# Gate and up projection: units 2 and 3 unit by unit, with their last products halved as in the later units

## The chip, the cores and the metric

The kernel runs on one core of a Trainium2 chip. The metric is the device time of one execution in microseconds (us). Five engines work side by side, each through a queue of its own in a fixed order: TensorE (PE in the profile; its weight loads are PEld), VectorE (DVE), ScalarE (ACT), GpSimd (POOL), and SyncE (SP), which here only issues transfers between HBM (the large memory) and SBUF (the on-chip memory). Matmuls write to PSUM banks, which DVE and ACT read. Engines wait for each other by semaphores.

## The reference

A two-layer encoder on 1024 tokens of width 1024, all in float32. Cut to what matters, one layer does this:

```
h = rmsnorm(x, norm_mix[i])
...                                      # attention (window or grid) and memory attention
x = x + concat(y_tok, y_mem) @ w_out[i]
h = rmsnorm(x, norm_ffn[i])
gu = h @ w_gate_up[i]                    # 1024 x 1024 times 1024 x 5632
x = x + (silu(gu[:, :2816]) * gu[:, 2816:]) @ w_down[i]
```

The change is in the product `h @ w_gate_up`, in both layers.

## The kernel before, in words

Every float32 operand of a matmul is split into a high and a low part. ACT casts the high part (`hi`, L107), DVE subtracts it from the original for the low part (`lo`, L110), and a product takes three matmuls: high by high, high by low, low by high (`three`). So each weight tile costs one ACT and one DVE instruction before TensorE can use it.

Gate and up work on 22 units `us[0..21]` (`Pair`), each 128 gate columns and 128 up columns. A unit's weights and the normalized input are cut into a two-by-two block product that is done with seven products instead of eight (n = 0 to 6 in the code; the words of the change count them from 1). One product is twelve 128x512 matmuls: four blocks of 128 rows by three terms. Right operands `B[n]` are common to all units: for n = 0, 1, 4, 5 they are the tiles `hB`, for n = 2, 3, 6 the tiles `hT8` (shown as `hT`), made by `right_sides` from the normalized x. Left operands are the unit's weights or sums of them, made by POOL (L1061, L1068) in the tile `wS` and then split into a tile of two products: n = 0 and 1 from the raw weights, n = 2 and 3 from the sums in `wS`, n = 4 and 5 from further sums. These overwrite `wS`, so POOL's second pair of subtractions waits until `lo` of the tile for 2 and 3 is done. `wS` has two buffers (tag `S`), the tiles for splits come from `wgu8` (six buffers, first four units, n = 0 and 1), from tag `whl` in lower SBUF (three buffers, shared with other stages) or from tag `w8` in upper SBUF (`wgu2`, one buffer). Products 0, 2, 4, 6 add up in a PSUM bank X, products 1, 3, 5 in a bank Y; after most of them ACT or DVE reads the bank (`read`), before the next product adds to it.

From the third pair on, product 6 of two neighbours is done jointly (`Fourth`): both left tiles and the right operand `B[6]` are halved once more, and seven products of half the rows and half the columns (six 128x256 matmuls each, L1186) take the place of two products of twelve 128x512 matmuls. They stand in three groups, A (two), B (two) and C (three), between the neighbour's last products, in a bank X4 and a bank Y4; DVE subtracts their results (L1214). The last product of C adds to the half of Y4 that DVE has read after B. `quarters` makes the quarter-size right operands (`q4`, `q4h`) and overwrites half of `B[6]`'s first tiles, so it runs when the undivided products 6 are done.

The list `order` fixes the sequence of products. The first four units do products 0 and 1 first, one unit after the other. Units 0 and 1, and then units 2 and 3, do n = 3, 2, 5, 4, 6 in turn, each for both units. The later ones go unit by unit. The loop `gate_up` walks the list; four places ahead of a product it calls `prepare`, which makes its left tile, and then it advances the generators for the right operands, `rest` (`right_sides`) and `more` (`quarters`).

While the first products run, the second half's norm is finished: TensorE adds squares (`st`, L223), DVE adds epsilon (`nv`, L243), POOL takes the power (`nr`, L244), DVE spreads it on a diagonal (`diag`, L252), and TensorE multiplies that by ones (`bc`, L266), after the first product of unit 1. DVE needs `bc` for the right operands of products 2 to 6.

The text fixes what is computed, in which tiles, and what follows what on a tile. The place of an instruction in its engine's queue is set at build time by a scheduler, which places an instruction where it reckons its inputs to be ready and its buffer to be free. On the chip each queue then runs strictly as built.

Of the kernel before, what the change touches and what calls it, by code (L numbers as in the profile page):

```python
# [41 lines left out]
def trunk_kernel(ctx: ExitStack, tc: tile.TileContext, a: dict, out: bass.AP):  # L42
# [63 lines left out]
    def hi(dst, src):  # L106
        return nc.scalar.copy(dst, src)  # L107

    def lo(dst, src, h, eng=None):
        return (eng or nc.vector).tensor_tensor(dst, src, h.bitcast(F32), op=ALU.subtract)  # L110
# [40 lines left out]
    def run_some(g, n):  # L151
        for _ in range(n):
            next(g, None)
# [388 lines left out]
    for layer in range(2):  # L542
# [470 lines left out]
        with (  # L1013
# [32 lines left out]
            class Pair:  # L1046
# [6 lines left out]
                def prepare(self, n):  # L1053

                    n -= n % 2
                    if n in self.left:
                        return
                    g1, g2 = self.raw[0][:, :HS], self.raw[0][:, HS:]
                    if n > 0:
                        u1, u2 = self.raw[1][:, :HS], self.raw[1][:, HS:]  # L1060
                    sub = lambda o, p_, q_: nc.gpsimd.tensor_tensor(o, p_, q_, op=ALU.subtract)  # L1061
                    s = self.raw[0]
                    if n == 2:
                        self.s = fs.tile([P, D], F32, tag="S", name="wS", bufs=2)
                    if n in (2, 4):
                        s = self.s
                    if n == 2:
                        nc.gpsimd.tensor_tensor(s[:, HS:], u1, u2, op=ALU.add)  # L1068
                        sub(s[:, :HS], s[:, HS:], g1)
                    if n == 4:  # L1070
                        sub(s[:, HS:], g1, u1)
                        sub(s[:, :HS], g2, s[:, :HS])
                    if n == 0 and self.j < first:
                        w = fp.tile([P, 2, D], F32R, tag="t8", name="wgu8", bufs=6)
                    elif n == 2 and self.j >= first:
                        w = fp.tile([P, 2, D], F32R, tag="w8", name="wgu2", bufs=1)
                    else:
                        w = wp.tile([P, 2, D], F32R, tag="whl", name="wgu", bufs=3)
                    if n == 6:
                        hi(w[:, 0, :HS], u2)  # L1080
                        lo(w[:, 1, :HS], u2, w[:, 0, :HS])
                    else:
                        hi(w[:, 0], s)
                        lo(w[:, 1], s, w[:, 0])
                    self.left[n], self.left[n + 1] = w[:, :, :HS], w[:, :, HS:]
                    if n == 4:
                        self.left[4], self.left[5] = self.left[5], self.left[4]
                    if n > 3 or (n == 0 and 2 <= self.j < first):
                        load_gu()
# [142 lines left out]
            first = 4  # L1232
            order = [(u, n) for u in us[:first] for n in (0, 1)]
            for j in range(0, NF, 2):
                a_, b_ = us[j : j + 2]
                z = Fourth(a_, b_)
                if j < first:
                    order += [(u, n) for n in (3, 2, 5, 4, 6) for u in (a_, b_)]
                else:
                    order += [(a_, n) for n in range(6)] + [(b_, n) for n in range(4)]  # L1240
                    order += [(z, "A"), (b_, 4), (z, "B"), (b_, 5), (z, "C")]

            loads = [(us[j], 0) for j in range(first)] + [(us[0], 1), (us[1], 1)]
# [3 lines left out]
            def load_gu():  # L1247
                u, i = next(loads, (None, 0))
                if u is not None:
                    u.raw[i] = raw_tile("wgu_raw")  # L1250
                    nc.sync.dma_start(u.raw[i], a["w_gu"][layer, 2 * u.j + i])
# [3 lines left out]
            for f in range(2):  # L1255
                for m in range(NK):
                    n = f * NK + m + 3
# [89 lines left out]
            def hand_over(p, a_, b_):  # L1347


                b11, b12, b21, b22 = a_.c2, a_.c1, b_.c2, b_.c1  # L1350
                sub = lambda p_, q_: nc.vector.tensor_tensor(o, p_, q_, op=ALU.subtract)
                keep(0, p, b11)
                keep(1, p, b21)
                keep(5, p, b22)
                o = t1 = temp("t1")
                sub(b12, b11)
                keep(3, p, t1)
                o = t2 = temp("t2")
                sub(b22, t1)
                keep(2, p, t2)  # L1360
                o = b12
                sub(b22, b12)
                keep(4, p, b12)
                o = temp("t4")
                sub(t2, b21)
                keep(6, p, o)
# [4 lines left out]
            def gate_up():  # L1371
                load_gu()
                for i, (u, n) in enumerate(order):
                    if i + lead < len(order):
                        v, n_ = order[i + lead]
                        v.prepare(n_)
                    u.product(n)
                    u.read(n)
                    if i == 1:
                        norms[1].sums()  # L1380
                    if i > 1:
                        run_some(rest, 2 if i == 2 or i >= 2 * first else 1)
                    if i >= 7 * first - 1:
                        run_some(more, 1)
                    if n == "C":
                        hand_over(u.units[0].j // 2, *u.units)
                    elif n == 6 and u.j % 2:
                        hand_over(u.j // 2, us[u.j - 1], u)
                    yield i - len(order)
# [215 lines left out]
            for to_go in gate_up():  # L1605
                for what, g in ahead.get(to_go, ()):
                    if what is keep_rows:
                        keep_rows(g)
                    elif what is left_side:
                        left_side(0, g, (us[-1].copied, us[-1].summed) if g == 1 else ())  # L1610
                    else:
                        what(0, g)
# [7 lines left out]
            for at_, (i, g) in enumerate(dorder):  # L1620
# [4 lines left out]
                p, n = groups[g]  # L1625
# [128 lines left out]
```

## Time and profile before

| | |
|---|---|
| median of 3 runs | 2112.03 us (2110.97 to 2112.73) |
| the profiled execution | 2112.72 us, its span 2110.9 us |
| TensorE busy in the span | 2092.0 us, 99% |
| VectorE, ScalarE, GpSimd busy | 72%, 51%, 28% |
| mean granted clock of TensorE | 0.998 of full |

How to read the rows shown below: a timeline row has the start in us from the span's beginning, the duration, engine, line of the kernel, operation, result and operands by the program's names without buffer numbers, shapes, and how many instructions are merged (x24); in brackets stands how long the engine had waited and for what. A matmul's shown duration includes its way through the array; two matmuls overlap, so the distance between starts is what PE spends. In a row of windows the columns are the stretch, its length, the busy time and count of PE, PEld, DVE, ACT and POOL, the granted clock, the share of the transfer engines and GB/s. Layer 0 has its gate and up products from 391 us on, layer 1 from 1463 us on.

### The profile page before, as it was taken

What the parts mean: (1) busy time and instruction counts of PE and PEld (TensorE: products, weight loads), DVE (VectorE), ACT (ScalarE), POOL (GpSimd) and SP (SyncE); (2) the same over time, 40 slices, a digit from 0 to 9 for tenths busy, and PEclk for the clock granted to TensorE, in tenths of its full rate; (3) what the DMA queues carried; (4) which work ended last, traced back from release to release, by engine and by line L of the source; (5) the groups of instructions that cost most, each with busy time, mean ns of one, the idle gap of its engine ahead of it and who ended that gap; (6) DMA issues with size and microseconds to landing.
All of it is one profiled execution on the core that took longest, in us unless ns stands there. A gap on an engine that the chain in (4) does not pass through costs nothing.

```text
span 2110.9 us, 29032 instructions
## 1 busy us (share of the span) xinstructions
PE 2092.0 (99%) x10318; PEld 1751.5 (83%) x10318; DVE 1524.3 (72%) x2474; ACT 1076.9 (51%) x2037; POOL 582.7 (28%) x615
## 2 busy tenths in 40 slices
PE   9999999999999999999999999999999999999998
PEld 8788888888888888888888888888788888888886
DVE  7787886897666666866766666677986666678675
ACT  6687785544334335444466666664543434344443
POOL 0344330334434430000233223203343444400001
PEclk9999999999999999999999999999999999999999
DMA  6421138232333227956232222274233333277562
GB/s 233 146 82 51 31 103 283 89 115 101 109 115 110 85 105 281 337 180 206 80 98 68 69 72 78 65 269 155 75 110 105 110 115 105 91 263 280 184 210 94
DMA packets 121776, 288.07 MB, mean 136 GB/s; under 512 B 12704, under 2 KB 21152, under 8 KB 121632
## 3 DMA queue, kind: packets, MB, share of 16 engines
q1 hardware_dynamic: 113744, 272.42, 38.5%
q10 hardware_dynamic: 7888, 13.79, 1.7%
q8 instruction: 82, 1.34, 0.3%
q14 instruction: 62, 0.51, 0.1%
HBM read 211.19 MB, written 68.95 MB: 133 GB/s over the span
## 4 chain that ended last, share of the span: by engine, by line
PE 80%; issue 12%; DVE 3%; POOL 2%; ACT 2%; DMA 1%; SPq 0%; POOLq 0%; ACTq 0%; DVEq 0%
PE X L1104 16%; PE Y L1104 16%; PE mm L141 15%; PE po L141 8%; PE X L1542 5%; PE Y L1542 4%; PE S L746 3%; PE O L812 3%; PE pT L791 3%; PE X L1186 2%; PE Y L1186 2%; PE mm L448 1%; POOL wS L1061 1%; POOL wf L110 1%; DVE wgu L110 0%
## 5 line engine op out<-in xcount | busy, mean ns | idle before, releaser
L1104 PE MATMUL Y<-hB,wgu 128*128 128x512 f32 x1056 | 255.6, 391 | 0.8 <-ACT c L1124 0.8
L1104 PE MATMUL X<-hB,wgu 128*128 128x512 f32 x1056 | 254.9, 391 | 0.0
L1542 PE MATMUL X<-hB,wd 128*128 128x512 f32 (+1 forms) x1092 | 242.9, 383 | 0.0
L110 DVE TENSOR_TENSOR wgu<-wS,wgu 128x1024 fp32r<-128x1024 f32 (+1 forms) x124 | 154.3, 1245 | 120.5 <-ACT wgu L107 120.4
L1542 PEld LDWEIGHTS X<-hB,wd 128*128 128x128 f32 x1092 | 200.2, 188 | 40.1 <-issue 0.5
L1104 PEld LDWEIGHTS Y<-hB,wgu 128*128 128x128 f32 x1056 | 196.8, 188 | 43.4 <-ACT c L1124 1.6
L1104 PEld LDWEIGHTS X<-hB,wgu 128*128 128x128 f32 x1056 | 195.9, 188 | 40.1 <-ACT g L1121 0.2
L776 POOL TENSOR_SCALAR p<-p,stat 128x384 f32<-128x384 f32 (+1 forms) x256 | 141.8, 573 | 302.5 <-DVE stat L773 196.7
L141 PE MATMUL mm<-hT,wqk 128*128 128x512 f32 x672 | 199.2, 405 | 0.0
L107 ACT CAST wgu<-wS 128x1024 fp32r<-128x1024 f32 (+1 forms) x124 | 114.3, 923 | 141.9 <-POOL wS L1061 124.5
L141 PE MATMUL po<-yT,wo 128*128 128x512 f32 x768 | 183.5, 394 | 0.0
L1542 PE MATMUL Y<-hB,wd 128*128 128x512 f32 x792 | 180.2, 389 | 0.0
L1542 PEld LDWEIGHTS Y<-hB,wd 128*128 128x128 f32 x792 | 148.7, 188 | 30.8
L244 POOL TENSOR_TENSOR nr<-nv,neg_half 128x4 f32<-128x4 f32 (+1 forms) x12 | 13.2, 1103 | 582.6 <-DVE nv L243 573.3
L141 PEld LDWEIGHTS po<-yT,wo 128*128 128x128 f32 x768 | 142.9, 188 | 29.1 <-DVE yT L110 0.2
L107 ACT CAST hB<-b_raw 128x512 fp32r<-128x512 f32 x154 | 89.7, 618 | 124.9 <-DMA b_raw<-b_d 108.0
L1104 PE MATMUL X<-hT,wgu 128*128 128x512 f32 x624 | 150.3, 391 | 0.0
L1061 POOL TENSOR_TENSOR wS<-wgu_raw 128x512 f32<-128x512 f32 x44 | 61.1, 1389 | 291.6 <-DVE wgu L110 291.6
L1104 PEld LDWEIGHTS X<-hT,wgu 128*128 128x128 f32 x624 | 116.9, 188 | 26.2
L762 ACT ACTIVATE p<-p,stat 128x256 f32<-128x256 f32 (+1 forms) x192 | 112.3, 586 | 48.7 <-DVE stat L758 47.1
L110 DVE TENSOR_TENSOR hB<-b_raw,hB 128x512 fp32r<-128x512 f32 x154 | 100.3, 689 | 49.8 <-ACT hB L107 49.6
L110 DVE TENSOR_TENSOR pl<-pT,ph 128x384 fp32r<-128x384 f32 (+1 forms) x256 | 119.2, 493 | 17.5 <-ACT ph L107 14.3
(201 smaller groups left out, 4248.3 us busy)
## 6 DMA issues: line engine op xcount, KB each, us to landing
wgu_raw<-in_w_gu SPq DMA_DIRECT2D x92, 512.0 KB, 3.6
b_raw<-b_d SPq DMA_DIRECT2D x70, 512.0 KB, 4.5
wd_raw<-in_w_dn SPq DMA_DIRECT2D x50, 512.0 KB, 4.5
b_d<-c SPq DMA_DIRECT2D x88, 256.0 KB, 2.1
b_d<-t SPq DMA_DIRECT2D x66, 256.0 KB, 2.2
wo_raw<-in_w_out SPq DMA_DIRECT2D x32, 512.0 KB, 3.7
wd_other<-in_w_dn SPq DMA_DIRECT2D x20, 512.0 KB, 7.3
xr_d<-x ACTq DMA_DIRECT2D x32, 256.0 KB, 2.9
```

Source lines behind the costliest of these rows:

```text
L107: return nc.scalar.copy(dst, src)
L110: return (eng or nc.vector).tensor_tensor(dst, src, h.bitcast(F32), op=ALU.subtract)
L141: nc.tensor.matmul(ps[:, :n], l, r, start=start and i == 0 and j == 0, stop=stop and i == len(order) - 1 and j == 2,)
L746: nc.tensor.matmul(s_[:, :n], Q[self.h][:, qb * P : (qb + 1) * P], k, start=j == 0, stop=j == 1)
L762: nc.scalar.activation(p[:, :n], p[:, :n], AF.Exp, bias=m1, scale=-1.0, accum_out=s1)
L776: nc.gpsimd.tensor_scalar(p[:, :n], p[:, :n], ri[:, i : i + 1], 1.0, op0=ALU.mult, op1=ALU.mult)
L791: nc.tensor.transpose(tr[:, j * P : (j + 1) * P], p[:, j * P : (j + 1) * P], ident)
L812: nc.tensor.matmul(o[:, c0 : c0 + w * P], self.value(j), t[:, s0 : s0 + w].rearrange("p j q -> p (j q)"), start=j == js[0] and t is self.p ...
L1061: sub = lambda o, p_, q_: nc.gpsimd.tensor_tensor(o, p_, q_, op=ALU.subtract)
L1104: nc.tensor.matmul(ps, l, r, start=n in (0, 1, 3, 6) and k == 0 and i == 0, stop=k == 3 and i == 2, skip_group_check=True,)
L1186: nc.tensor.matmul(bank[:, at : at + h2], l, r, start=start and k == 0 and i == 0, stop=stop and k == 1 and i == 2, skip_group_check=True,)
L1542: nc.tensor.matmul(bank[:, c], l, r, start=i in (0, 1, 3, 6) and p == 0 and n == 0, stop=p == HF - 1 and n == 2, skip_group_check=True,)
```

## The change

Units 2 and 3 leave the interleaved form and go unit by unit: after their early products 0 and 1 unit 2 does 2 to 5, unit 3 does 2 and 3, and then come A, 4, B, 5 and C as in the later pairs. Their two products 6 become the seven of half size. Their left tile for products 2 and 3 comes from tag `w8`. `quarters` starts after product 15 of the list instead of 27.

```diff
-                    elif n == 2 and self.j >= first:
+                    elif n == 2 and self.j >= 2:
                         w = fp.tile([P, 2, D], F32R, tag="w8", name="wgu2", bufs=1)
...
-                if j < first:
+                if j == 0:
                     order += [(u, n) for n in (3, 2, 5, 4, 6) for u in (a_, b_)]
                 else:
-                    order += [(a_, n) for n in range(6)] + [(b_, n) for n in range(4)]
+                    alone = 2 if j < first else 0
+                    order += [(a_, n) for n in range(alone, 6)] + [(b_, n) for n in range(alone, 4)]
                     order += [(z, "A"), (b_, 4), (z, "B"), (b_, 5), (z, "C")]
...
-                    if i >= 7 * first - 1:
+                    if i >= 2 * first + 7:
                         run_some(more, 1)
```

The queues move with it. The first place is POOL's queue in layer 0 around the norm's `nr` (layer 1 has the same). Numbers behind names tell buffers apart: `wS_4827` is the sum tile of unit 2, `wS_4851` (after: `wS_4931`) that of unit 3. Before:

```order
L1061 TENSOR_TENSOR wS_4608<-wgu_raw_4264,wS_4608 128x512
L1068 TENSOR_TENSOR wS_4827<-wgu_raw_4681 128x512
L1061 TENSOR_TENSOR wS_4827<-wS_4827,wgu_raw_4493 128x512
L244 TENSOR_TENSOR nr_4532<-nv_4531,neg_half_112 128x4
L1068 TENSOR_TENSOR wS_4851<-wgu_raw_4780 128x512
L1061 TENSOR_TENSOR wS_4851<-wS_4851,wgu_raw_4711 128x512
```

And after:

```order
L1061 TENSOR_TENSOR wS_4608<-wgu_raw_4264,wS_4608 128x512
L1068 TENSOR_TENSOR wS_4827<-wgu_raw_4681 128x512
L1061 TENSOR_TENSOR wS_4827<-wS_4827,wgu_raw_4493 128x512
L1061 TENSOR_TENSOR wS_4827<-wgu_raw_4493,wgu_raw_4681 128x512
L1061 TENSOR_TENSOR wS_4827<-wgu_raw_4493,wS_4827 128x512
L244 TENSOR_TENSOR nr_4532<-nv_4531,neg_half_112 128x4
L1068 TENSOR_TENSOR wS_4931<-wgu_raw_4780 128x512
```

The two subtractions that make unit 2's second sums have moved from behind the next unit's to ahead of `nr`.

The second place is DVE's queue at the same moment. `wgu2_4830` is unit 2's left tile for products 2 and 3, `g1_4508` the gate of unit 0. Before:

```order
L230 TENSOR_TENSOR sq_4218<-sq_4218,sq_4485 128x512
L230 TENSOR_TENSOR sq_4169<-sq_4169,sq_4218 128x512
L1112 TENSOR_TENSOR g1_4508<-Y_4510,g1_4508 128x512
L243 TENSOR_SCALAR nv_4531<-st_4526 128x4
L252 TENSOR_TENSOR diag_4535<-ident_106,nr_4532 128x512
```

And after:

```order
L230 TENSOR_TENSOR sq_4218<-sq_4218,sq_4485 128x512
L230 TENSOR_TENSOR sq_4169<-sq_4169,sq_4218 128x512
L110 TENSOR_TENSOR wgu2_4830<-wS_4827,wgu2_4830 128x1024
L1112 TENSOR_TENSOR g1_4508<-Y_4510,g1_4508 128x512
L243 TENSOR_SCALAR nv_4531<-st_4526 128x4
L252 TENSOR_TENSOR diag_4535<-ident_106,nr_4532 128x512
```

The low part of unit 2's left tile now stands ahead of `nv`; its cast on ACT has moved up to right behind the copy of `g1_4508`. `bc` keeps its place in TensorE's queue.

The third place is DVE's queue at the end of units 2 and 3. `wgu2_5119` and `wgu_5176` are tiles of unit 4, `c1_5010` and `c1_5099` the up halves of units 2 and 3, `X4_5068` and `Y4_5069` the banks of the half products. Before, the end of these units read their undivided products:

```order
L1112 TENSOR_TENSOR c1_5040<-c1_5040,X_4589 128x512
L1112 TENSOR_TENSOR c2_4957<-c2_4957,g2_4985 128x512
L1112 TENSOR_TENSOR c1_5040<-c1_5040,g1_4602 128x512
L1323 TENSOR_TENSOR x_3895<-x_3895 128x256
L110 TENSOR_TENSOR wgu_5117<-wS_5060,wgu_5117 128x1024
L1112 TENSOR_TENSOR c1_5056<-c1_5056,X_4635 128x512
```

And after:

```order
L1112 TENSOR_TENSOR c2_4968<-c2_4968,g2_4949 128x512
L1214 TENSOR_TENSOR c1_5010<-c1_5010,X4_5068 128x256
L1214 TENSOR_TENSOR c1_5010<-c1_5010,Y4_5069 128x256
L110 TENSOR_TENSOR wgu2_5119<-wS_5116,wgu2_5119 128x1024
L1214 TENSOR_TENSOR c1_5010<-c1_5010,X4_5068 128x256
L110 TENSOR_TENSOR wgu_5176<-wS_5116,wgu_5176 128x1024
L1112 TENSOR_TENSOR c2_5066<-c2_5066,c1_5099 128x512
L1214 TENSOR_TENSOR c1_5099<-c1_5099,Y4_5069 128x256
```

Two splits of unit 4 now stand among the reads of the half products, the second one ahead of the read of `Y4` after B.

## The prediction

> **What bounds the kernel now.** I read the page's busy times first.
>
> ```profile
> span 2110.9 us, 29032 instructions
> PE 2092.0 (99%) x10318; PEld 1751.5 (83%) x10318; DVE 1524.3 (72%) x2474; ACT 1076.9 (51%) x2037; POOL 582.7 (28%) x615
> ```
>
> PE (TensorE) is busy for 99% of the span, so the time falls only if PE gets less to do and rises by whatever PE has to wait. The profiled execution took 2112.72 us, 1.8 around the span and 0.7 above the median of 2112.03; a difference under 0.2% (4.2 us) cannot be told from none. Then I read the timeline of PE in layer 0, from the products of units 2 and 3 to the halves of the next pair. Columns: start, duration, engine, line, operation; the distance between starts is what PE spends.
>
> ```profile
> 443.35 5.76 PE L1104 MATMUL Y<-hT,wgu 128*128 128x512 f32 x24
> 448.95 5.77 PE L1104 MATMUL X<-hT,wgu 128*128 128x512 f32 x24
> 455.09 5.82 PE L1104 MATMUL Y<-hB,wgu 128*128 128x512 f32 x24 [0.37 <-ACT c L1124]
> 460.75 5.60 PE L1104 MATMUL X<-hB,wgu 128*128 128x512 f32 x24
> 466.19 5.75 PE L1104 MATMUL X<-hT,wgu 128*128 128x512 f32 x24
> 471.78 2.90 PE L1104 MATMUL X<-hB,wgu 128*128 128x512 f32 x12
> 474.51 2.89 PE L1104 MATMUL Y<-hB,wgu 128*128 128x512 f32 x12
> ...
> 499.04 0.88 PE L1186 MATMUL X<-hT,wgu 128*128 128x256 f32 x6
> 499.75 0.88 PE L1186 MATMUL Y<-hT,wgu 128*128 128x256 f32 x6
> ```
>
> The ten products of units 2 and 3 take 443.35 to 471.78, 28.43 us, with one small wait in them. A later unit's product takes 2.73 (471.78 to 474.51) and one half-size product 0.72 (499.04 to 499.75; I take 0.72).
>
> **PE's own work: a gain of 1.55 us per layer.** Now these units issue eight products at 2.73 (21.84) and seven halves at 0.72 (5.04): 26.88, against 28.43. In it lie product 7 (5.59 from 466.19 to 471.78, now 5.04); the products on hT, which cost 5.60 a pair in row 443.35 and whose left tile now comes from upper SBUF as in the later units; and the waits before and in row 455.09 (5.66 against 5.44 for row 460.75). If PE never waits, that is 3.1 us in two layers.
>
> **The norm's chain moves behind preparation work: a loss of 4.3 us per layer.** The new left tile of unit 2 has a buffer of its own that nothing holds, so the split of wgu2_4830 and the POOL subtractions behind it are now issued before the second norm's statistics. The timeline there, before the change:
>
> ```profile
> 396.63 1.60 POOL L1061 TENSOR_TENSOR wS<-wS,wgu_raw 128x512 f32<-128x512 f32 x1
> ...
> 398.24 0.17 DVE L243 TENSOR_SCALAR nv<-st 128x4 f32<-128x4 f32 x1 [0.54 <-PE st L223]
> 398.48 1.02 POOL L244 TENSOR_TENSOR nr<-nv,neg_half 128x4 f32<-128x4 f32 x1 [0.26 <-DVE nv L243]
> 399.54 0.69 DVE L252 TENSOR_TENSOR diag<-ident,nr 128x512 f32<-128x512 f32 x1 [1.14 <-POOL nr L244]
> ...
> 400.93 1.02 PE L266 MATMUL bc<-diag,ones 128*128 128x512 f32 x2
> ...
> 1468.12 1.61 POOL L1061 TENSOR_TENSOR wS<-wS,wgu_raw 128x512 f32<-128x512 f32 x1
> ...
> 1472.57 1.02 PE L266 MATMUL bc<-diag,ones 128*128 128x512 f32 x2
> ```
>
> POOL finished the first half of wS_4827 at 398.23 and turned to nr at once; diag was ready at 400.23, and PE took bc at 400.93, when its product ended: 0.7 us of slack, and every matmul behind bc queues on it. For the prices of the inserted steps and for the second term I take the timeline of units 4 and 5, which already work in the new form:
>
> ```profile
> 482.69 2.89 PE L1104 MATMUL X<-hB,wgu 128*128 128x512 f32 x12
> ...
> 483.89 1.05 ACT L107 CAST wgu<-wS 128x1024 fp32r<-128x1024 f32 x1
> 484.98 1.23 DVE L110 TENSOR_TENSOR wgu<-wS,wgu 128x1024 fp32r<-128x1024 f32 x1 [0.17 <-ACT wgu L107]
> ...
> 486.29 1.80 POOL L1061 TENSOR_TENSOR wS<-wgu_raw 128x512 f32<-128x512 f32 x1 [9.38 <-DVE wgu L110]
> ...
> 488.05 1.74 POOL L1061 TENSOR_TENSOR wS<-wgu_raw,wS 128x512 f32<-128x512 f32 x1
> ...
> 491.19 1.21 DVE L110 TENSOR_TENSOR wgu<-wS,wgu 128x1024 fp32r<-128x1024 f32 x1
> ...
> 492.48 1.67 POOL L1068 TENSOR_TENSOR wS<-wgu_raw 128x512 f32<-128x512 f32 x1 [2.70 <-DVE wgu L110]
> ...
> 494.23 1.62 POOL L1061 TENSOR_TENSOR wS<-wS,wgu_raw 128x512 f32<-128x512 f32 x1
> ...
> 495.81 2.28 POOL L1068 TENSOR_TENSOR wS<-wgu_raw 128x512 f32<-128x512 f32 x1
> ...
> 498.17 1.28 POOL L1061 TENSOR_TENSOR wS<-wS,wgu_raw 128x512 f32<-128x512 f32 x1
> ...
> 501.01 1.22 DVE L110 TENSOR_TENSOR wgu<-wS,wgu 128x1024 fp32r<-128x1024 f32 x1
> ...
> 502.31 1.29 POOL L1061 TENSOR_TENSOR wS<-wgu_raw 128x512 f32<-128x512 f32 x1 [2.87 <-DVE wgu L110]
> ...
> 503.56 1.30 POOL L1061 TENSOR_TENSOR wS<-wgu_raw,wS 128x512 f32<-128x512 f32 x1
> ...
> 505.97 1.23 DVE L110 TENSOR_TENSOR wgu<-wS,wgu 128x1024 fp32r<-128x1024 f32 x1 [1.41 <-ACT wgu L107]
> ...
> 507.90 0.42 DVE L1214 TENSOR_TENSOR c<-c,Y 128x256 f32<-128x256 f32 x1
> ...
> 508.85 0.88 PE L1186 MATMUL Y<-hT,wgu 128*128 128x256 f32 x6
> ```
>
> Now, from 398.23: ACT's cast 1.05 and DVE's subtraction 1.23, with 0.03 before each (484.98 follows 483.89 + 1.05), end at 400.57. POOL's second half may overwrite wS only then: 0.08 later, and 2.55 (502.31 to 504.86, DVE idle) to 3.5 (486.29 to 489.79, DVE busy). So nr starts at 403.2 to 404.15 instead of 398.48. Its 1.02 and diag's 0.69, with 0.1 between, give bc at 405.0 to 405.95: PE waits 4.1 to 5.0 us. In layer 1 POOL's first half ends at 1469.73, and the same steps give 1476.5 to 1477.45 against 1472.57: 3.9 to 4.9. DVE has one subtraction (g1) there and then waits for nr itself, which is nearer to the idle price: I take 4.4 and 4.2, 4.3 on average. DVE's nv waits behind the inserted subtraction too, but ends long before POOL is free. Everything after bc hangs on bc in either kernel and moves with it.
>
> **The pair's serial chain gets less time: a loss of 3.6 us per layer.** One buffer (w8) holds the left tile for products 3 and 4, so unit 3's can be cast only when unit 2's product 4 has ended. From there runs one chain: cast and subtract, two POOL subtractions into wS, cast and subtract (ends 492.40), two POOL operations for the next unit, its cast and subtract (501.01), two POOL subtractions, cast and subtract (505.97 to 507.20), and only behind that in DVE's queue the subtraction (507.90) that frees the half bank for the last of the seven products (508.85). In units 4 and 5 it took 482.69 to 508.32, 25.6 us, and PE needed 26.16 (482.69 to 508.85) for what it does meanwhile: it just fitted. Units 2 and 3 have no products 1 and 2 here, so PE does 6 x 2.73 + 6 halves at 0.72 = 20.7 us. The chain may be shorter where it waited for PE: the subtraction at 501.01 sat behind A's results; without that, POOL's pair from 495.81 (free at 499.45) would have let it end some 2.8 earlier, at 22.8. It may be longer, since its start now shares DVE with the quarter-size right sides. So PE waits 2.1 to 4.9 us; I take 3.6, above the middle for that reason.
>
> Costed at nothing: the extra POOL sums, splits and small reads of the halves, which lie in the chain just priced or beside PE; the quarter-size operands, issued earlier, whose first user is product A; and SP's loads, four for these units as before, with unit 3's second load released by POOL rather than DVE and so earlier. If DVE falls behind there, PE loses up to a microsecond more at product 5.
>
> **The sum.** Per layer 4.3 + 3.6 - 1.55 = 6.35; two layers 12.7. On the profiled execution 2125.4, on the median 2124.7: I say 2125.
>
> A wait of this length has no row in this trace with dense matmuls after it. What there is lies at the end, where PE does little after 2098:
>
> ```profile
> 2095.00:2100.00 5.00, 4.83 (x39) 4.62 (x37) 4.02 (x12) 1.67 (x4) 0.41 (x1) 1.00 0.01 3
> 2100.00:2103.00 3.00, 1.37 (x4) 1.18 (x4) 2.24 (x7) 0.00 (x0) 0.69 (x1) 0.60 0.56 191
> ```
>
> The granted clock (third number from the right) falls from 1.00 to 0.60 within a few microseconds of thin work. [...]
>
> **Rivals.**
> - *The clock falls in the waits.* If PE then runs at half speed for as long as it waited (3.6 to 4.3), it loses 2 us at each of four places: 2125 + 8 = 2133. For it: the two rows above. Against it: the waits last no longer than the thin work after which it fell. 0.13.
> - *Only the norm's wait appears*, since ACT and DVE run ahead in the pair and the chain closes up to 20.7: 2112.0 + 2 x (4.3 - 1.55) = 2117.5. For it: parts of the 25.6 waited for PE. 0.15.
> - *Only the pair's wait appears*: 2112.0 + 2 x (3.6 - 1.55) = 2116.1. 0.03.
> - *Not slower: the change does what it says.* It decides at nr: if POOL's inserted pair ended so early that nr slipped by no more than the 0.7 of slack, and the chain fitted, PE would keep its 3.1: 2108.9, just within 0.2%. Against it, cast, subtraction and two POOL operations cannot take under 4.8. 0.10, of which 0.03 for a gain beyond 0.2%.
>
> **How the numbers follow.** My forecast has 0.59; with both bounds of both terms it alone spans 2 x (3.9 + 2.1 - 1.55) = 8.9 to 2 x (5.0 + 4.9 - 1.55) = 16.7 above the median, 2121 to 2129. To leave out no more than 2 in 10 the range reaches down to 2116 and up to 2133. Slower by over 0.2%: 0.59 + 0.15 + 0.13 = 0.87; within 0.2%: 0.07 and the pair's wait alone, 0.10; faster 0.03.
>
> **What would show it.** In the waits of PE, bc on diag with some 4.3 us in each layer, and nr on POOL behind two more L1061 rows. L1186 has ten pairs of 42 matmuls in each layer instead of nine, at the same pitch. In units 2 and 3 PE waits for the c subtraction (L1214) before the last half product. If bc starts within a microsecond of its product's end, the first term is wrong; if the last half product follows at once, the second is; a granted clock under 1.00 behind either adds the clock. I am most wrong if the inserted work runs at times other than these rows, since one term rests on POOL's queue alone.

## The result, and the profile after

The changed kernel takes 2125.6 us (median of 6 runs, 2124.3 to 2128.7) against 2111.9 for the kernel before (6 runs on the same chip): a ratio of 1.0069, 95% interval 1.0058 to 1.0079. It is slower by 13.7 us, where 13 were forecast. The profiled execution of the changed kernel was the longest of its six (2128.7), so its trace holds some 3 us more than a median run.

The page's span and busy times after the change:

```profile
span 2126.9 us, 29152 instructions
PE 2096.0 (99%) x10354; PEld 1756.0 (83%) x10354; DVE 1517.6 (71%) x2488; ACT 1079.1 (51%) x2041; POOL 607.0 (29%) x623
```

PE is busy 4.0 us longer although its matmuls need less time at full speed (26.89 us a pair in the last kernel below, 28.43 before with a wait of 0.37 in it), and it waits longer too. The view of waits by engine names the places (columns: total us, times, longest):

```profile
PE bc L266 <- DVE diag L252: 9.2, 4, 3.8
PE Y L1186 <- DVE c L1214: 4.2, 2, 2.1
...
PE X L1186 <- DVE c L1214: 1.1, 3, 0.5
```

Before, bc waited 1.8 us in all, and c never held a half product for more than 0.2. The timeline of TensorE at the second norm in layer 0 before the change:

```profile
398.06 3.03 PE L1104 MATMUL X<-hB,wgu 128*128 128x512 f32 x12
...
401.39 3.35 PE L1104 MATMUL Y<-hB,wgu 128*128 128x512 f32 x12
404.57 2.95 PE L1104 MATMUL X<-hB,wgu 128*128 128x512 f32 x12
```

The same place after the change, and bc in layer 1:

```profile
397.51 3.04 PE L1104 MATMUL X<-hB,wgu 128*128 128x512 f32 x12
397.70 1.05 ACT L107 CAST wgu<-wS 128x1024 fp32r<-128x1024 f32 x1 [3.56 <-POOL wS L1061]
398.78 1.23 DVE L110 TENSOR_TENSOR wgu<-wS,wgu 128x1024 fp32r<-128x1024 f32 x1 [2.24 <-ACT wgu L107]
...
400.08 1.27 POOL L1061 TENSOR_TENSOR wS<-wgu_raw 128x512 f32<-128x512 f32 x1 [2.42 <-DVE wgu L110]
...
401.32 1.26 POOL L1061 TENSOR_TENSOR wS<-wgu_raw,wS 128x512 f32<-128x512 f32 x1
402.54 1.02 POOL L244 TENSOR_TENSOR nr<-nv,neg_half 128x4 f32<-128x4 f32 x1
...
404.34 2.07 PE L266 MATMUL bc<-diag,ones 128*128 128x512 f32 x2 [3.78 <-DVE diag L252]
405.42 4.24 PE L1104 MATMUL Y<-hB,wgu 128*128 128x512 f32 x12
409.50 2.71 PE L1104 MATMUL X<-hB,wgu 128*128 128x512 f32 x11
...
1483.94 2.07 PE L266 MATMUL bc<-diag,ones 128*128 128x512 f32 x2 [3.56 <-DVE diag L252]
```

Cast, VectorE's subtraction and two POOL rows stand ahead of nr. From the start of X to bc it is 6.83 us (397.51 to 404.34), where it was 2.87 (398.06 to 400.93): 3.96 lost. In layer 1 it is 6.60 (from 1477.34) against 2.88 (1469.69 to 1472.57): 3.72 lost. The product behind bc then takes 4.08 (405.42 to 409.50) instead of 3.18 (401.39 to 404.57). The timeline of the last halves of units 2 and 3 in layer 0:

```profile
442.73 8.51 PE L1104 MATMUL X<-hT,wgu 128*128 128x512 f32 x36
...
469.51 0.97 PE L1186 MATMUL X<-q4h,wgu 128*128 128x256 f32 x6 [0.48 <-DVE c L1214]
...
473.99 1.05 ACT L107 CAST wgu<-wS 128x1024 fp32r<-128x1024 f32 x1 [6.55 <-POOL wS L1061]
474.95 0.58 ACT L1129 COPY c<-X 128x512 f32<-128x512 f32 x1
475.07 1.23 DVE L110 TENSOR_TENSOR wgu<-wS,wgu 128x1024 fp32r<-128x1024 f32 x1 [3.40 <-ACT wgu L107]
...
476.99 0.42 DVE L1214 TENSOR_TENSOR c<-c,Y 128x256 f32<-128x256 f32 x1
...
477.47 0.98 PE L1186 MATMUL Y<-hT,wgu 128*128 128x256 f32 x6 [2.08 <-DVE c L1214]
478.29 4.50 PE L1104 MATMUL X<-hB,wgu 128*128 128x512 f32 x12
482.63 2.91 PE L1104 MATMUL Y<-hB,wgu 128*128 128x512 f32 x12
```

The first row holds two products of the pair before (5.60 us) and unit 2's first. So the eight products and seven halves take 448.33 to 478.29, 29.96 us, where 26.88 would do without a wait: some 3.07 lost, of which 2.08 and 0.48 are the two waits shown; the rest lies in the starts just around them. In layer 1 it is the same (1529.04 to 1558.99, 29.95). The next product takes 4.34 (478.29 to 482.63) instead of 2.73. The view by stretches says why (third number from the right: granted clock):

```profile
406.00:410.00 4.00, 4.00 (x16) 3.08 (x15) 3.55 (x6) 1.23 (x2) 0.00 (x0) 0.84 0.00 0
478.00:484.00 6.00, 6.00 (x22) 4.84 (x22) 5.97 (x10) 1.22 (x2) 2.92 (x3) 0.72 0.17 64
1486.00:1490.00 4.00, 4.00 (x13) 3.10 (x12) 3.95 (x7) 1.22 (x2) 0.00 (x0) 0.58 0.00 0
1556.00:1562.00 6.00, 3.92 (x21) 3.30 (x21) 5.91 (x9) 1.82 (x4) 4.54 (x4) 1.00 0.22 82
```

The clock is low behind both waits on bc (0.84 and 0.58) and behind the pair's wait in layer 0 (0.72), and full behind the pair's wait in layer 1 (1.00). In this execution that adds some 1.5 + 2.6 + 1.6 us (each from the starts of the rows behind the wait, against the same rows before). The sum of the trace: 7.68 + 6.14 of waits, 5.7 of low clock, less 3.1 of saved matmuls, 16.4; the span grew by 16.0.

### The profile page after: what moved, and what is told of

It is laid out like the page before. It is cut to its first block, busy times and chain, and to the rows that moved or that the text cites. A ratio compares the mean times of both kernels' runs of the same rounds, so it can differ in the third digit from the quotient of the medians.

```text
span 2126.9 us, 29152 instructions
## 1 busy us (share of the span) xinstructions
PE 2096.0 (99%) x10354; PEld 1756.0 (83%) x10354; DVE 1517.6 (71%) x2488; ACT 1079.1 (51%) x2041; POOL 607.0 (29%) x623
## 5 line engine op out<-in xcount | busy, mean ns | idle before, releaser
L1061 POOL TENSOR_TENSOR wS<-wgu_raw 128x512 f32<-128x512 f32 x44 | 59.4, 1351 | 289.0 <-DVE wgu L110 289.0
L1104 PE MATMUL X<-hT,wgu 128*128 128x512 f32 x576 | 138.4, 391 | 0.0
L1068 POOL TENSOR_TENSOR wS<-wgu_raw 128x512 f32<-128x512 f32 x44 | 86.4, 1963 | 157.7 <-DVE wgu L110 132.9
```

Source lines behind the costliest of these rows:

```text
L1104: nc.tensor.matmul(ps, l, r, start=n in (0, 1, 3, 6) and k == 0 and i == 0, stop=k == 3 and i == 2, skip_group_check=True,)
```

## The experiments

All times are medians; the kernel before ran beside each group (2111.2, 2111.2, 2111.3), and the intervals are of the ratio to it. "Queued behind" means that the instruction is put behind another on its own engine and nothing else is asked for; the scheduler then places the rest.

| kernel | us | ratio to before, 95% interval |
|---|---|---|
| norm first | 2117.4 | 1.0029, 1.0019 to 1.0039 |
| norm first, own buffer for unit 3 | 2122.9 | 1.0054, 1.0041 to 1.0066 |
| upper tile alone, old order | 2122.0 | 1.0049, 1.0036 to 1.0061 |
| changed, norm's wait filled | 2124.1 | 1.0061, 1.0048 to 1.0073 |
| norm first, unit 4's split queued | 2110.8 | 1.0001, 0.9992 to 1.0010 |
| POOL's two rows behind nr only | 2125.1 | 1.0064, 1.0051 to 1.0076 |
| left tiles in the old pool | 2132.4 | 1.0101, 1.0085 to 1.0116 |
| the same, unit 4's split queued | 2129.0 | 1.0084, 1.0070 to 1.0098 |
| unit 4's split queued only | 2121.9 | 1.0046, 1.0032 to 1.0059 |
| the same, norm's wait filled | 2118.9 | 1.0040, 1.0027 to 1.0052 |
| three subtractions queued | 2110.9 | 1.0000, 0.9991 to 1.0009 |

**The norm first.**

```diff
-            nc.vector.tensor_tensor(
+            self.ready = nc.vector.tensor_tensor(      # diag
...
+                        if n == 2 and self.j == 2:
+                            queued.enter_context(tc.issue_after(norms[1].ready.ins))
```

> The split of unit 2's left tile is queued behind the norm's diag on VectorE, so nr goes ahead of the two subtractions on POOL; all else is as in the changed kernel. Theory (the norm's chain waits only because that work was put ahead of it): bc starts within 0.7 us of its product's end again, 3.96 + 3.72 = 7.7 us go, with the stretches of low clock behind them (1 to 4 us): 2125.6 becomes 2114 to 2117, and the waits of 2.1 and 0.5 us per layer before the halves of units 2 and 3 stay. Rival (the norm is late for another reason, such as its statistics): bc still waits 3.7 to 4.0 us, 2125.6. Rival (the work is needed early): units 2 and 3 now wait for the tile instead, 2120 or more.

Its timeline at the norm:

```profile
399.94 1.02 PE L266 MATMUL bc<-diag,ones 128*128 128x512 f32 x2
```

bc starts 2.88 us after X (397.06), as before the change, and 8.2 us go, which leaves the time 0.4 above the range expected. The wait on c stays (4.2 us, 2 times, as in the changed kernel). The work that was put ahead of nr is the cause of the norm's wait, and not of the pair's.

**The upper tile alone**, in the kernel before:

```diff
-                    elif n == 2 and self.j >= first:
+                    elif n == 2 and (self.j >= first or self.j == 2):
```

> The kernel before with one part of the change alone: unit 2's left tile takes the buffer in upper SBUF; order and product 7 are the old ones. Theory (the tile's free buffer alone lets the split run ahead of the norm): bc waits 3.7 to 4.0 us in each layer, with 1 to 4 us of low clock behind: 2111.9 becomes 2120 to 2123.5. Rival (the order unit by unit is what brings the split forward): bc waits under 1 us, 2111.6.

```profile
403.53 1.35 PE L266 MATMUL bc<-diag,ones 128*128 128x512 f32 x2 [3.79 <-DVE diag L252]
```

This is layer 0. In layer 1 the wait shown on bc is only 2.24 us, not the 3.7 to 4.0 expected, but there X itself took longer, since the clock fell soon after it had begun (0.76 from 1474 to 1478, 0.81 from 1478 to 1482), behind a wait of 1.02 us before the sums of squares (`st`). From the start of X to bc it is 6.84 us in both layers (396.69 to 403.53, 1475.58 to 1482.42), some 3.96 more than before. The old order with one tile moved loses 10.8 us: the free buffer alone is enough to let the split run ahead, without the order unit by unit.

**Only POOL's two rows behind nr.** The prediction let the first term rest on POOL's queue alone. Here the two subtractions of unit 2 follow nr on POOL, and the cast and VectorE's subtraction stay where they are:

```diff
+                            if self.j == 2:
+                                queued.enter_context(tc.issue_after(norms[1].power.ins))
                             sub(s[:, HS:], g1, u1)
                             sub(s[:, :HS], g2, s[:, :HS])
```

> The changed kernel with only POOL's two subtractions of unit 2 queued behind nr; ScalarE's cast and VectorE's subtraction stay ahead of nv. Theory of the prediction (POOL's queue alone makes nr late): bc starts within 0.7 us of its product's end, as with the norm first: 2117.4. Rival (VectorE's queue makes nv late as well: nv ended at 400.06 in the changed kernel): nr starts near 400.3 and bc near 402.2, 1.6 us after its product's end, in both layers: 2 x 2.2 us less wait than the changed kernel, 2119 to 2121, with or without a fall of the clock.

```profile
400.73 1.02 POOL L244 TENSOR_TENSOR nr<-nv,neg_half 128x4 f32<-128x4 f32 x1 [3.09 <-DVE nv L243]
...
401.78 1.75 DVE L252 TENSOR_TENSOR diag<-ident,nr 128x512 f32<-128x512 f32 x1 [1.14 <-POOL nr L244]
...
403.58 2.07 PE L266 MATMUL bc<-diag,ones 128*128 128x512 f32 x2 [3.07 <-DVE diag L252]
```

Both theories miss the time. The wait falls only from 3.78 and 3.56 to 3.07 in both layers: nr now waits for nv, which stands behind the inserted subtraction on VectorE (it ends at 400.65 here and at 400.67 in the changed kernel, not at 400.06), and diag, which now runs beside POOL's subtractions, takes 1.75 us where it took 0.69. The rival had the first of these and not the second.

**Unit 4's split behind unit 3's copy and subtraction**, with the norm first:

```diff
+                        if n == 4 and self.j == 4:
+                            queued.enter_context(tc.issue_after(us[3].copied.ins))   # ScalarE
+                            queued.enter_context(tc.issue_after(us[3].summed.ins))   # VectorE, frees Y4
```

> The norm first as before, and the cast and VectorE subtraction of unit 4's left tile (wgu_5176) queued behind unit 3's copy of product 4 on ScalarE and behind the subtraction that frees the half bank on VectorE. Theory (the last halves wait only because that split stands ahead of these two in the queues): the 2.1 us wait on c goes in both layers, and with it a stretch of low clock in some executions; 2117.4 becomes 2111 to 2113, and the 0.5 us wait before the halves of product B stays. Rival (the freeing subtraction is late for another reason, such as the copies ahead of it): the wait shrinks by less than 1 us, 2116 to 2117. Rival (the split is now late for its own user or for POOL): a new wait of over 1 us in unit 4, 2114 or more.

```profile
463.52 0.59 ACT L1135 COPY c<-X 128x512 f32<-128x512 f32 x1 [1.68 <-PE X L1110]
...
466.62 0.41 DVE L1220 TENSOR_TENSOR c<-c,Y 128x256 f32<-128x256 f32 x1
...
468.80 1.05 ACT L107 CAST wgu<-wS 128x1024 fp32r<-128x1024 f32 x1 [4.69 <-POOL wS L1061]
469.63 0.88 PE L1192 MATMUL Y<-hT,wgu 128*128 128x256 f32 x6
```

The last half product starts without a wait, 6.5 us go against the norm first alone, and the kernel is level with the one before. So the chain from the single buffer through casts, POOL and subtractions did not have to end before the last half product. It did because one cast stood ahead of unit 3's copy on ScalarE, and its subtraction ahead of the sum on VectorE. Which of the two alone would have held PE was not tried.

**Unit 3's left tile in another buffer**, with the norm first: unit 2's stays in upper SBUF, unit 3's goes to the pool of three.

> As the kernel with the norm first, and unit 3's left tile goes to the pool of the other left tiles, so that it need not wait until unit 2's product 4 has ended; unit 2's keeps the buffer in upper SBUF. Theory (the single buffer starts the pair's chain late): the waits before the halves of units 2 and 3 go too, 3.07 us per layer less than with the norm first alone; against the kernel before only the saved matmuls are left, 2 x 1.55 less some 0.3 for the tile's place: 2109 to 2110. Rival (the chain is bound by VectorE's and POOL's queues, not by the buffer): the 2.1 us wait on the c subtraction stays, 2114 to 2117.

```profile
447.94 2.03 PE L1107 MATMUL X<-hT,wgu 128*128 128x512 f32 x8
...
453.12 1.04 ACT L107 CAST wgu<-wS 128x1024 fp32r<-128x1024 f32 x1 [9.23 <-POOL wS L1061]
...
454.70 5.15 PE L1107 MATMUL X<-hB,wgu 128*128 128x512 f32 x12 [4.73 <-ACT g L1124]
```

Neither theory has this. The wait on c is gone from the view of waits, but the cast for which ScalarE now waits on POOL stands ahead of unit 2's copy of X, and PE loses 4.7 us in each layer at product 4 instead: 5.5 us slower than with the norm first alone. The edit moved more than the buffer: TensorE's own queue now has eight of the twelve matmuls of unit 3's product 2 (447.94) ahead of unit 2's product 4, in both layers. So the run shows that the block moved to another place. It does not show what the buffer alone would do in the old order of products.

**Both left tiles in the old pool** (`elif n == 2 and self.j >= first:` again, order and halves as changed), and the same with unit 4's split queued:

> The changed kernel with the left tiles of products 3 and 4 of units 2 and 3 in the old pool of three buffers: unit by unit and the halves stay, the tile in upper SBUF goes. Theory (the free tile is what brings the split ahead of the norm): bc waits under 1 us; the wait on c before the last halves stays, since unit 4's cast still stands ahead of unit 3's copy on ScalarE: 2114 to 2118. Rival (order and halves bring the split forward): bc waits 3.7 us, 2122 to 2126. Rival (three buffers are too few for units in this order): new waits on left tiles, 2120 or more.

> As the kernel with the tiles in the old pool, and unit 4's split behind unit 3's copy and subtraction. Theory: neither wait is left, only the matmuls saved, less 4 products a layer at 2.79 instead of 2.73: 2111.2 - 3.1 + 0.5 + about 1 for the waits of 0.5 before product B: 2109 to 2110.5. Rival (buffers too few): the same new waits as without the queueing.

The waits of the first:

```profile
PE X L1104 <- ACT g L1121: 8.4, 4, 3.7
PE X L1104 <- DVE wgu L110: 5.3, 2, 2.7
```

The norm waits no more (bc 1.8 us in all, as before), and the 2.1 us wait on c is gone as well, which the theory did not expect. But PE waits for left tiles (wgu), 2.7 us in each layer, and for copies: 2132.4, the slowest of all. Queueing unit 4's split takes 3.4 us off and leaves those waits (7.0 and 5.3). The time is that of the third rival, but its reason, too few buffers, is not shown. Here too TensorE's queue has work of unit 3 ahead of unit 2's product 4, and the left tile that PE waits for had been cast by 444.88; its subtraction stood behind reads and quarter-size operands in VectorE's queue:

```profile
450.15 1.21 DVE L110 TENSOR_TENSOR wgu<-wS,wgu 128x1024 fp32r<-128x1024 f32 x1
```

So without the extra tile the order unit by unit is slower still in the queues as built; whether three buffers could do in another order stays open.

**The norm's wait filled.** Sixteen extra matmuls are written into bc's own bank ahead of bc and overwritten by it, so that PE works through the wait without shortening it:

```diff
+            for l, r in fill:
+                nc.tensor.matmul(bc, l, r, start=True, stop=True)
```

> The changed kernel with 16 more matmuls of 128x512 into bc's own bank ahead of bc (their sums are overwritten), some 3.6 us of PE work in the wait of each layer; the wait is filled, not shortened. Theory (the clock falls because PE is idle there): bc starts when it did, the granted clock stays near 1.00 behind it, and 1 to 4 us of the 2125.6 go: 2121.5 to 2124.5. Rival (the falls there have another cause): clock 0.67 to 0.81 behind bc again, 2125.6 or up to 1 more.

```profile
399.78 3.88 PE L267 MATMUL bc<-hB,wgu 128*128 128x512 f32 x16
...
403.79 1.13 PE L268 MATMUL bc<-diag,ones 128*128 128x512 f32 x2
404.35 3.34 PE L1106 MATMUL Y<-hB,wgu 128*128 128x512 f32 x12
407.53 2.96 PE L1106 MATMUL X<-hB,wgu 128*128 128x512 f32 x12
```

bc comes 6.89 us after X (396.90), as in the changed kernel, yet the product behind it takes 3.18 again, not 4.08, at a granted clock of 1.00 (403 to 410). The time fell by 1.5, inside the range given but near its small end. The pair's waits may have hidden part of the gain: in this profiled execution the clock fell behind both of them (0.82 from 478 to 484, 0.77 from 1556 to 1562). So the pair's wait was taken out and the test done again, unfilled and filled:

> The changed kernel with only unit 4's split queued behind unit 3's copy and subtraction: the norm's wait stays, the pair's goes. Theory (the two terms add, and the clock's price comes on top): 2110.8 of the kernel with both queued, plus 3.96 + 3.72 us of wait, plus 3 us of low clock behind them: 2120.5 to 2122.5. Rival (no price of the clock): 2118.5. Rival (the pair's split behind the copies helps only where the norm goes first): 2125.6.

> The same with the 16 overwritten matmuls into bc's bank ahead of bc, so that PE works through the wait. Theory (the clock falls because PE is idle, and costs 3 us in two layers): bc starts when it did, granted clock 1.00 behind it in both layers, 2118 to 2119, 2 to 4 us below the unfilled one. Rival (low clock is not from the idle wait): as the unfilled one.

The view by stretches of the unfilled, then of the filled kernel:

```profile
404.00:410.00 6.00, 5.50 (x11) 3.69 (x12) 3.83 (x7) 1.22 (x2) 0.00 (x0) 0.50 0.23 80
1482.00:1489.00 7.00, 6.43 (x14) 4.42 (x15) 4.83 (x8) 1.22 (x2) 0.00 (x0) 0.52 0.21 70
```

```profile
404.00:410.00 6.00, 6.00 (x24) 4.59 (x25) 4.84 (x8) 1.22 (x2) 0.00 (x0) 1.00 0.17 67
1479.00:1486.00 7.00, 6.88 (x28) 4.95 (x27) 5.30 (x9) 1.22 (x2) 0.45 (x1) 1.00 0.25 75
```

With the same lateness of bc, 2121.9 and 2118.9: PE's idleness cost 3.0 us beyond the wait. The medians carry this with some doubt (2118.6 to 2125.2 and 2117.9 to 2121.7, five runs each, and their two intervals overlap); the clock columns do not. The unfilled kernel's profiled execution was its longest, so its columns show more than a median run. All its runs bear the price out, though: ordered by time they are ordered by mean granted clock too, from 2118.6 us at 0.998 to 2125.2 at 0.994. The fastest lies at the 2118.5 that the first rival gave for no price of the clock.

**A third subtraction queued** (unit 4's first left tile behind the sums of product A), on top of the other two:

> The kernel with the norm first and unit 4's split queued, and VectorE's subtraction of unit 4's first left tile also queued behind the two that free the banks of product A. Theory: the wait of 0.5 us before the halves of product B goes in both layers: 2109.8 to 2110.4, 0.5 to 1 us below the kernel with both queued, which the intervals can hardly tell. Rival (that subtraction was not what held them): the wait stays, 2110.8.

```profile
1508.24 8.51 PE L1112 MATMUL X<-hT,wgu 128*128 128x512 f32 x36
...
1534.39 0.88 PE L1194 MATMUL X<-q4h,wgu 128*128 128x256 f32 x6
...
1540.73 2.91 PE L1112 MATMUL X<-hB,wgu 128*128 128x512 f32 x12
```

The 0.5 us waits before the halves of product B are gone. In layer 1 the first row holds two products of the pair before (5.60 us) and unit 2's first, so this pair takes 1513.84 to 1540.73, 26.89 us. The time, 2110.9, does not show it. No version was measurably faster than the kernel before.

## Why the prediction was right, point by point

- **PE's own work, 26.88 us a pair: right.** The last kernel, with no wait left in the pair, took 26.89. But the 3.1 us over two layers did not come out as a measurable gain: the two kernels without the waits stand 0.3 to 0.4 below the one before, with intervals of about 2 us either way. Other small waits took a part (1.5 us on ScalarE's copies of g2, three times, in the last kernel's view of waits); the rest of the difference stays open.
- **The norm's chain, 4.3 us a layer: right in place and cause, somewhat too large.** It measured 3.96 and 3.72. The step that was mis-sized is POOL's pair: 2.55 to 3.5 was taken, and nr followed after 2.46 (400.08 to 402.54), with little on VectorE beside the pair. That "one term rests on POOL's queue alone" was wrong: with POOL's queue cleared, VectorE's queue and a slower diag held bc for 3.07.
- **The pair's serial chain, 3.6 us a layer: right in place, too large, and only partly right in cause.** It measured 3.07. The prediction saw VectorE's queue; the copy on ScalarE behind the cast was missed, and the length of the chain was not what bound: queueing one split differently removed the long wait, with the single buffer left as it was.
- **The sum: close partly by luck.** Without the clock the terms measured give 7.7 + 6.1 - 3.1 = 10.7 us, not 12.7. A median run lost 13.7. The remaining 3.0 equals what the norm's wait cost in clock where it was tried alone, though the run-to-run spread allows 1 to 4, and the pair's wait adds to it in some executions. So two terms taken too large made up for a clock that the sum left out.
- **The rival "the clock falls in the waits": partly what happened,** in three of four places of the profiled execution, at 1.5 to 2.6 us each, not four times 2. It came on top of smaller waits instead of on top of the forecast. The half speed that it supposed is in the traces: the granted clock is 0.50 from 2101 to 2103 us of the kernel before, and in the changed kernel from 403.89 to 407.30, from 478.98 to 482.39 and from 1482.50 to 1489.33. That it lasts as long as the wait is shown by no run: behind the wait of 3.78 us it lasted 3.41 us, behind that of 3.56 it lasted 6.83, behind one of 2.08 again 3.41. The clock fell behind shorter waits too: behind those of 3.07 us in both layers of the kernel with only POOL's rows moved (0.75 from 404 to 410, 0.72 from 1482 to 1488), and behind four of the eight waits of 2.1 us.
- **Only one of the two waits, or none:** 2117.5 and 2116.1 were priced without any clock. The norm's wait alone gave 2121.9 (against 2117.5) and the pair's alone 2117.4 (against 2116.1); each was over its price. "Not slower" needed both queues in another order; with them it came out level, at 2110.8.

## What to carry to other kernels

A tile with a free buffer let its preparation start early here, and the early work stood ahead of urgent work on ScalarE, VectorE and POOL, so that bc came 3.96 and 3.72 us later: before giving a step a buffer, read in the order what it will overtake on ScalarE, VectorE and POOL, and queue it behind what PE waits for. Here both long waits went when the work ahead of the late instruction was queued behind it. Another buffer for the same tile changed TensorE's own order too and brought a dearer wait (4.73 us instead of 2.08), so after such an edit read all the queues again. And price a new idle stretch of PE like the two on bc (3.78 and 3.56 us) at its length plus the 1.5 and 2.6 us that the low clock behind them cost in the changed kernel's trace.

## What the runs showed of the hardware that was not expected

- The granted clock fell behind four of the eight waits of about 2.1 us in four profiled kernels: in layer 0 of the changed kernel (0.72 from 478 to 484) and not in layer 1 (1.00 from 1556 to 1562); with the norm first in layer 1 (0.95 from 1548 to 1556; the product behind the wait took 4.33 us, 1545.14 to 1549.47) and not in layer 0 (1.00 from 470 to 484); with the norm's wait filled in both layers (0.82 and 0.77); with only POOL's rows moved in neither (1.00 from 470 to 484 and from 1548 to 1562). Behind the seven waits of 3.07 to 3.80 us on bc it fell every time: the changed kernel (0.50 from 403.89 and from 1482.50), the upper tile alone in layer 0 (0.72 from 403 to 406), only POOL's rows moved (0.75 and 0.72), and unit 4's split queued only (0.50 and 0.52). In the changed kernel's profiled execution the falls and rises between 20 and 2095 us are at 403.89, 407.30, 478.98, 482.39, 1482.50 and 1489.33: the later ones follow the first by 1, 22, 23, 316 and 318 times 3.413 us. In the 3.41 us before each of the three falls PE was busy for 0.07, 1.51 and 1.29 us. Of this kernel's two waits of 2.08 us, the first (475.39 to 477.47) lies almost wholly in such a stretch, and the clock fell at its end; the second (1556.09 to 1558.17) lies across a boundary of the same steps (1557.60), with PE busy for 1.91 us in the stretch before it and 2.83 in the one behind, and the clock did not fall. That this place decides is the author's reading of one trace, and no run tried it. The view by stretches, first for the one and then for the other:

```profile
475.57:478.98 3.41, 1.51 (x9) 1.38 (x10) 3.32 (x5) 1.53 (x2) 2.60 (x3) 1.00 0.35 137
1554.18:1557.60 3.42, 1.91 (x15) 1.62 (x13) 1.82 (x2) 2.48 (x3) 1.00 (x2) 1.00 0.47 153
```

- With sixteen matmuls whose sums are overwritten in bc's wait, the granted clock was 1.00 in both layers (403 to 410 and 1482 to 1490 in the changed kernel filled, 404 to 410 and 1479 to 1486 with the norm's wait alone).
- A VectorE operation took over twice its time beside POOL subtractions: diag 0.69 us without them (in the kernel before and in the changed one), 1.75 with POOL's rows at 401.72 and 402.94 beside it, in the kernel with only POOL's rows moved.
